# Local attention by token halves, two heads a step, with half of the output projection moved beside it

## The chip, the core and the metric

The kernel runs on one core of one Trainium2 chip. The time is the device time of one launch in microseconds, and the number compared is the median over several runs. The engines are called by the names of the profile: PE (TensorE, with PEld for its weight loads), DVE (VectorE), ACT (ScalarE), POOL (GpSimd) and SP (SyncE, which here only starts transfers).

## What is computed

One decoder layer over 512 tokens of width 1024, in float32. The part that matters here is the end of the attention block and the start of the feed-forward block:

```python
mix = concatenate([moba, nsa, diff, swa], axis=-1)   # 4 groups of 4 heads of 64
x = x + rms_norm(mix @ w_out, attn_post_norm)
h = rms_norm(x, ffn_pre_norm)
x = x + rms_norm(conv_ffn(h, w_gate, w_up, ...), ffn_post_norm)
```

`swa` is attention over a band: a query sees itself and the 127 tokens before it, there are two key/value heads for four query heads, and a learned "sink" joins the maximum and the sum of each softmax row. With query tiles of 128 tokens, tile i needs the key tiles i-1 and i; tile 0 needs only key tile 0.

## The kernel before

Every float32 operand of a matmul is split into a high and a low part, and a product is three matmuls (`mm3`, lines 405 to 407: high by high, high by low, low by high). The split costs an ACT copy and a DVE or POOL subtraction for each block; for weights these are `Weights.operand` (lines 191 and 194, tiles `wu`, and `wa` for the first two operands of the feed-forward block) and `Weights.plain` (152, 157). Line 177 is a sum or difference of weight blocks on POOL, made for a seven-product (Strassen) form of the gate and up projections, and it overwrites blocks that the splits of `wa` read.

Attention is written as a list of tasks, one for each head (swa, moba), head and branch (nsa) or head pair (diff). A task has steps: scores of a query tile with the softmax exponent (line 948 on DVE, 949 on ACT), `end` (row sums, reciprocal, normalisation on POOL, line 941), `transposes` (PE 973, ACT 976, DVE 977), and `pv` (values; for swa line 1139). After `pv`, `fold` adds two partial results (ACT 994, DVE 995) and, after every second head, `mix_pair` splits the mixed output into `mixT` (ACT 999, POOL 1000). The steps are sorted by a hand-written due time. Between them a generator, `everything()`, supplies projection work in pieces of three matmuls (`fill`, `advance`): first the input projections, last `fill_out`, the half of the output projection whose inputs are the moba and nsa heads (k = 0 to 3), kept in eight tiles `part[t][n]` (four token tiles t, two column halves n).

After the last swa task the second half of the output projection follows: `out_rest(t, n)` (12 matmuls in a PSUM bank, tags `mm` and `sc`, then a DVE addition into `part`, line 1217), for t = 0, 1, then `second_norm(0)` and `second_norm(1)`, then t = 2, 3 and their norms. `second_norm` is: two squares with row sums on ACT (1225), a scalar on DVE (1228), a power on POOL (1231), a product with the gain (1241, POOL except for t = 0), the residual addition into `x1` (1244, DVE), again square, scalar (1230) and power, and the second gain (1247, DVE). `right_operand` transposes the result (PE 1257) and splits it (ACT 1259, DVE 1260). Two operands of the first token half ("11", "21") feed the four products of `first_products` (lines 1312 to 1314, 24 matmuls each); all others need both halves and come from differences (1284).

A scheduler of the framework orders the instructions of each engine by a simulated time with the program order as priority; a `high_priority` block raises the priority. Tiles of one tag are handed out in the order in which the program asks for them. The tag "H" has 16 tiles: the normalised input, later `mixT` 4 to 7 and `wa`. The pool `fp`, which holds `x1`, uses the memory of the attention pools and so can be written only after the last swa task has read its probabilities.

## Time and profile before

| | us |
|---|---|
| median of 3 runs | 822.89 |
| lowest, highest run | 821.38, 822.95 |
| the profiled execution, its own time | 821.32 |
| its span (first to last instruction) | 819.5 |

The profile shows one execution. Busy time of an engine is the sum of its instructions; a bracket with an arrow in a timeline is idle time of the engine before the instruction, and what ended it. The mean granted TensorE clock over the span was 0.984 of full speed.

### The profile page before, as it was taken

The page shows a single profiled execution, that of the slowest core. Times are in us where ns is not written, and L with a number is a line of the kernel's source. Part 1 is how long each engine was busy: PE and PEld are TensorE (multiplying, and loading weights), DVE is VectorE, ACT ScalarE, POOL GpSimd, SP SyncE. Part 2 cuts the span into 40 slices and gives each one's busy share as a digit, 9 for nine tenths or more (in the row PEclk, how much of TensorE's full clock was granted, in tenths as well). Part 3 has the DMA queues.
Part 4 walks back from the last instruction along what each step waited for, and adds up shares of the span by engine and source line. Part 5 has one row for each costly group of instructions (what it writes and reads, how often), then busy time and mean ns, then how long its engine had stood idle before and what let it go on. Part 6 is the DMA issues. An engine that isn't in the chain of part 4 may idle for free.

```text
span 819.5 us, 13505 instructions
## 1 busy us (share of the span) xinstructions
PE 781.0 (95%) x5087; PEld 712.1 (87%) x5087; DVE 665.6 (81%) x1131; ACT 446.9 (55%) x931; POOL 338.5 (41%) x309
## 2 busy tenths in 40 slices
PE   8999998999989769999999999999999999999995
PEld 8998986997868658988998998998998998998984
DVE  5657768877586999896797797897897987989857
ACT  6657666777676545645554453454454454445532
POOL 5245333336244757343343441461561561563103
PEclk9999999999989979999999999999999999999998
DMA  7455201416211403412114305216116026033212
GB/s 213 121 149 138 64 22 46 129 52 216 80 52 52 154 7 109 145 61 94 52 50 157 103 10 197 67 38 206 43 61 206 18 86 205 1 104 104 69 60 102
DMA packets 72920, 78.76 MB, mean 96 GB/s; under 512 B 7782, under 2 KB 58136, under 8 KB 72856
## 3 DMA queue, kind: packets, MB, share of 16 engines
q1 hardware_dynamic: 71032, 73.71, 29.3%
q10 hardware_dynamic: 1824, 4.20, 1.5%
q8 instruction: 40, 0.66, 0.3%
q14 instruction: 24, 0.20, 0.1%
HBM read 73.71 MB, written 2.10 MB: 93 GB/s over the span
## 4 chain that ended last, share of the span: by engine, by line
PE 57%; DVE 33%; issue 3%; DMA 3%; ACT 2%; POOL 1%; ACTq 0%; DVEq 0%; POOLq 0%
DVE wu L194 13%; PE mm L405 5%; PE mm L406 5%; PE mm L407 4%; DVE y L1362 3%; PE mm L1312 3%; PE mm L1314 3%; PE mm L1313 3%; PE tr L406 3%; PE tr L407 2%; PE sc L1314 2%; PE sc L1313 2%; PE sc L1312 2%; PE tr L405 2%; PE tr L973 2%
## 5 line engine op out<-in xcount | busy, mean ns | idle before, releaser
L194 DVE TENSOR_TENSOR wu<-pair,wu 128x512 fp32r<-128x512 f32 x188 | 174.6, 964 | 15.8 <-ACT wu L191 15.6
L191 ACT ACTIVATE wu<-pair 128x512 fp32r<-128x512 f32 x188 | 108.6, 622 | 76.3 <-PE sc L1314 19.8
L1314 PE MATMUL mm<-fT,wu 128*128 128x256 f32 x488 | 138.3, 283 | 0.7 <-DVE wu L194 0.7
L1312 PE MATMUL mm<-fT,wu 128*128 128x256 f32 x488 | 138.2, 283 | 0.7 <-ACT mo L1343 0.7
L1313 PE MATMUL mm<-fT,wu 128*128 128x256 f32 x488 | 138.2, 283 | 0.0
L1314 PE MATMUL sc<-fT,wu 128*128 128x256 f32 x392 | 111.3, 284 | 0.0
L1313 PE MATMUL sc<-fT,wu 128*128 128x256 f32 x392 | 111.1, 284 | 0.0
L1312 PE MATMUL sc<-fT,wu 128*128 128x256 f32 x392 | 111.0, 284 | 0.0
L152 ACT ACTIVATE wu<-raw 128x512 fp32r<-128x512 f32 (+2 forms) x126 | 71.3, 609 | 67.9 <-DMA raw<-in_ffn_w_down_dram 43.8
L177 POOL TENSOR_TENSOR sum<-pair 128x512 f32<-128x512 f32 x32 | 48.7, 1526 | 141.2 <-DMA pair<-in_ffn_w_up_dram 71.4
L177 POOL TENSOR_TENSOR pair<-sum,pair 128x512 f32<-128x512 f32 x32 | 56.2, 1771 | 116.6 <-DVE wu L194 114.7
L177 POOL TENSOR_TENSOR pair<-pair 128x512 f32<-128x512 f32 x64 | 103.4, 1628 | 2.0
L157 DVE TENSOR_TENSOR wu<-raw,wu 128x512 fp32r<-128x512 f32 (+2 forms) x96 | 73.5, 783 | 35.3 <-ACT wu L152 34.8
L1312 PEld LDWEIGHTS mm<-fT,wu 128*128 128x128 f32 x488 | 93.6, 192 | 1.2 <-ACT mo L1343 0.9
L1314 PEld LDWEIGHTS mm<-fT,wu 128*128 128x128 f32 x488 | 93.6, 192 | 0.9 <-DVE wu L194 0.9
L1313 PEld LDWEIGHTS mm<-fT,wu 128*128 128x128 f32 x488 | 93.6, 192 | 0.3
L941 POOL TENSOR_SCALAR P<-P,rc 128x128 f32<-128x128 f32 (+2 forms) x80 | 42.3, 547 | 84.3 <-DVE rc L1039 39.6
L1313 PEld LDWEIGHTS sc<-fT,wu 128*128 128x128 f32 x392 | 75.2, 192 | 0.3
L1312 PEld LDWEIGHTS sc<-fT,wu 128*128 128x128 f32 x392 | 75.2, 192 | 0.3
L1314 PEld LDWEIGHTS sc<-fT,wu 128*128 128x128 f32 x392 | 75.3, 192 | 0.0
L949 ACT ACTIVATE P<-P,mn 128x128 f32<-128x128 f32 (+2 forms) x96 | 52.1, 543 | 33.2 <-DVE mn L948 32.8
L157 POOL TENSOR_TENSOR wu<-raw,wu 128x512 fp32r<-128x512 f32 (+2 forms) x30 | 40.6, 1356 | 48.4 <-ACT wu L152 44.7
(318 smaller groups left out, 1955.8 us busy)
## 6 DMA issues: line engine op xcount, KB each, us to landing
pair<-in_ffn_w_gate_dram SPq DMA_DIRECT2D x16, 1024.0 KB, 7.7
pair<-in_ffn_w_up_dram SPq DMA_DIRECT2D x16, 1024.0 KB, 5.4
raw<-in_ffn_w_down_dram SPq DMA_DIRECT2D x32, 512.0 KB, 4.1
raw<-in_w_in_dram SPq DMA_DIRECT2D x14, 512.0 KB, 3.9
raw<-in_w_out_dram SPq DMA_DIRECT2D x8, 512.0 KB, 5.4
raw<-in_w_in_dram SPq DMA_DIRECT2D x10, 256.0 KB, 3.2
x<-in_x_dram SPq DMA_DIRECT2D x4, 512.0 KB, 4.6
x<-in_x_dram ACTq DMA_DIRECT2D x4, 512.0 KB
```

The costliest lines, as they stand in the source:

```text
L152: keep(self.nc.scalar.activation(box["h"][:, sl], box["r"][:, sl], AF.Copy))
L157: keep(eng.tensor_tensor(box["l"][:, sl], box["r"][:, sl], f32(box["h"][:, sl]), op=ALU.subtract))
L177: self.nc.gpsimd.tensor_tensor(block(g, out), block(g, a), block(g, b), op=op)
L191: self.nc.scalar.activation(box["h"][g], block(g, src), AF.Copy)
L194: self.nc.vector.tensor_sub(box["l"][g], block(g, src), f32(box["h"][g]))
L405: pe.matmul(o, lh, rh, start=first, stop=False)
L406: pe.matmul(o, lh, rl, start=False, stop=False)
L407: pe.matmul(o, ll, rh, start=False, stop=last)
L949: act.activation(pi, pi, AF.Exp, bias=mn[:, i:i + 1], scale=-1.0, accum_out=sm[:, i:i + 1])
L1312: pe.matmul(o, wh, rh, start=first, stop=False, skip_group_check=True)
L1313: pe.matmul(o, wh, rl, start=False, stop=False, skip_group_check=True)
L1314: pe.matmul(o, wl, rh, start=False, stop=last, skip_group_check=True)
```

## The change

The four swa tasks are now pairs (token half, pair of heads) in the order (0,0), (0,1), (1,0), (1,1): each does two query tiles of two heads. Scores, exponents and normalisation keep their shapes; `end` uses two small activations for the sinks; the transposes are 3 + 3 tiles for the first token half and 4 + 4 for the second; `pv` puts both heads into one PSUM bank; the folds are 64 rows by 256 columns, and the mixed output is split by halves of 256 tokens, the last one on DVE. After the pair (0,1) the filler goes on with `fill_rest`: it loads the residual input of token tiles 0 and 1 through SP into four "H" tiles, takes the four weight units of `out_rest`, and yields the pieces of `out_rest` for t = 0, 1, with their additions put into the queue of side work. `x1` is loaded from memory only for t = 2, 3, and `second_norm(0)` and `(1)` read the early copy. `out_rest` uses the `mm` banks alone. For t = 2, 3 it runs after the attention, as before.

```diff
--- before.py
+++ after.py
@@ -885,18 +885,45 @@
                 mm_done()
         yield "out"
 
+    def out_rest(t, n):
+        ps = mm_bank()
+        sl = slice(128 * t, 128 * t + 128)
+        for k in range(4):
+            w = late["wo"][2 * n + k // 2]
+            mm3(ps, mixT[0][4 + k][:, sl], mixT[1][4 + k][:, sl], w[0][:, k % 2, :], w[1][:, k % 2, :], k == 0, k == 3)
+            yield 1
+        later(lambda: vec.tensor_add(part[t][n], part[t][n], ps))
+        mm_done()
+
+    def fill_rest():
+
+        late["x"] = [[f32(tt("xm", "H")) for _ in range(2)] for _ in range(2)]
+        for t in range(2):
+            for n in range(2):
+                sp.dma_start(late["x"][t][n], x[0, 128 * t:128 * t + 128, 512 * n:512 * n + 512])
+        late["wo"] = [W.take() for _ in range(4)]
+        for n in range(2):
+            for t in range(2):
+                yield from out_rest(t, n)
+        yield "rest"
+
     def everything():
         yield from fill_moba()
         yield from fill_nsa()
         yield from fill_diff()
         yield from fill_swa()
         yield from fill_out()
+        while not late.get("half"):
+            yield "wait"
+        yield from fill_rest()
 
     filler = everything()
     seen = set()
 
     def advance():
         y = next(filler, None)
+        if y == "wait":
+            return None
         if isinstance(y, str):
             later(lambda: seen.add(y))
         elif y is not None and side:
@@ -1106,42 +1133,63 @@
         t.pv = pv
         return t
 
-    def swa_task(h):
+    def swa_task(half, p):
+
         t = Task()
-        p, a = h // 2, h % 2
         box = []
-        score = stacked_score(sq_[h], sk[p], late["skl"][p])
-
-        def one(i):
-            if i == 0:
-                box.append(new_probs())
-            P, mn, sm = box[0]
-            probs(score, slope(3, h), i, P, mn, sm, SOFF, SN, sbias[:, 256 - SN[i]:256], 128 * max(i - 1, 0),
-                  nsink[:, h:h + 1])
-        t.first = [lambda i=i: one(i) for i in range(4)]
+        ns = ((128, 256), (256, 256))[half]
+        w = ns[0] + ns[1]
+        at = [w * (j // 2) + ns[0] * (j % 2) for j in range(4)]
+
+        def one(j):
+            if j == 0:
+                box.extend(new_probs())
+            P, mn, sm = box
+            a, i, n = j // 2, 2 * half + j % 2, ns[j % 2]
+            ps = bank("sc")
+            stacked_score(sq_[2 * p + a], sk[p], late["skl"][p])(ps, i, 128 * max(i - 1, 0), n)
+            pi = P[:, at[j]:at[j] + n]
+            vec.tensor_tensor_reduce(pi, ps[:, 0:n], sbias[:, 256 - n:256], slope(3, 2 * p + a),
+                                     nsink[:, 2 * p + a:2 * p + a + 1], ALU.add, ALU.min, mn[:, j:j + 1])
+            act.activation(pi, pi, AF.Exp, bias=mn[:, j:j + 1], scale=-1.0, accum_out=sm[:, j:j + 1])
+        t.first = [lambda j=j: one(j) for j in range(4)]
 
         def end():
-            t.P, mn, sm = box[0]
+            t.P, mn, sm = box
             es = st1.tile([128, 4], F32, tag="es", name=nm("es"))
-            act.activation(es, mn, AF.Exp, bias=sink[:, h:h + 1])
+            for a in range(2):
+                h = 2 * p + a
+                act.activation(es[:, 2 * a:2 * a + 2], mn[:, 2 * a:2 * a + 2], AF.Exp, bias=sink[:, h:h + 1])
             vec.tensor_add(sm, sm, es)
-            normalise(t.P, recip(sm), SOFF, SN)
+            normalise(t.P, recip(sm), at, ns + ns)
         t.end = end
-        t.srcs = SWA
+        t.srcs = [[w * a + 128 * n for n in range(w // 128)] for a in range(2)]
 
         def pv():
             o = bank("pv")
             v = vcs["s"]
-            for j, c, n, first in ((0, 0, 256, True), (1, 0, 128, False), (2, 0, 256, True), (1, 128, 128, False),
-                                   (3, 0, 128, False)):
-                for b in range(2):
-                    oc = 128 * j + c
-                    pe.matmul(o[:, oc:oc + n], v[:, j, p, 64 * a:64 * a + 128],
-                              t.pt[b][:, 256 * j + c:256 * j + c + n], start=first and b == 0,
-                              stop=not first and b == 1, skip_group_check=True)
-            fold(o, h, 3)
-            if a:
-                mix_pair(mos[3], 6 + p)
+            mo = ta("mo", MO)
+            steps = (((0, 0, 256, 0), (1, 128, 128, 256)), ((2, 0, 256, 128), (1, 0, 128, 0), (3, 128, 128, 384)))[half]
+            for a in range(2):
+                for n, (j, c, m, pc) in enumerate(steps):
+                    for b in range(2):
+                        pe.matmul(o[:, 256 * a + c:256 * a + c + m], v[:, j, p, 64 * a:64 * a + 128],
+                                  t.pt[b][:, w * a + pc:w * a + pc + m], start=n == 0 and b == 0,
+                                  stop=n == len(steps) - 1 and b == 1, skip_group_check=True)
+            tmp = ta("tmp", TMP)
+            for a in range(2):
+                r, c = 64 * a, slice(256 * a, 256 * a + 256)
+                act.activation(tmp[r:r + 64, 0:256], o[64 - r:128 - r, c], AF.Copy)
+                vec.tensor_add(mo[r:r + 64, 0:256], o[r:r + 64, c], tmp[r:r + 64, 0:256])
+            if half == 0:
+                mixT[0][6 + p], mixT[1][6 + p] = tt("mixh", "H"), tt("mixl", "H")
+            c = slice(256 * half, 256 * half + 256)
+            act.activation(mixT[0][6 + p][:, c], mo[:, 0:256], AF.Copy)
+            (vec if half and p else pool).tensor_tensor(mixT[1][6 + p][:, c], mo[:, 0:256], f32(mixT[0][6 + p][:, c]),
+                                                        op=ALU.subtract)
+            if p and not half:
+                fill_to("out")
+                late["half"] = True
         t.pv = pv
         return t
 
@@ -1151,7 +1199,7 @@
             (None, moba_task, [(h,) for h in range(4)], RATES[0], "moba"),
             ("nsa", nsa_task, [(h, b) for h in range(4) for b in range(2)], RATES[1], None),
             ("diff", diff_task, [(h,) for h in range(4)], RATES[2], None),
-            ("swa", swa_task, [(h,) for h in range(4)], RATES[3], None)):
+            ("swa", swa_task, [(a, p) for a in range(2) for p in range(2)], RATES[3], None)):
         for n, ar in enumerate(args):
             box = {}
 
@@ -1193,28 +1241,18 @@
         cur = rate or cur
         with tc.high_priority(HP):
             f()
-    fill_to("out")
+    fill_to("rest")
     ph_cm.__exit__(None, None, None)
     first_half.close()
 
 
     fp = ctx.enter_context(tc.tile_pool(name="fp", bufs=1))
     x1 = [fp.tile([128, D], F32, name=f"x1_{t}") for t in range(4)]
-    for t in range(4):
+    for t in (2, 3):
         act.dma_start(x1[t], x[0, 128 * t:128 * t + 128, :])
     t2pool = ctx.enter_context(tc.tile_pool(name="t2", bufs=XB))
     gpost, gpre = gains[0][:, 0, :], gains[0][:, 1, :]
-
     flush()
-    ws = [W.take() for _ in range(4)]
-
-    def out_rest(t, n):
-        ps = bank(("mm", "sc")[n])
-        sl = slice(128 * t, 128 * t + 128)
-        for k in range(4):
-            w = ws[2 * n + k // 2]
-            mm3(ps, mixT[0][4 + k][:, sl], mixT[1][4 + k][:, sl], w[0][:, k % 2, :], w[1][:, k % 2, :], k == 0, k == 3)
-        vec.tensor_add(part[t][n], part[t][n], ps)
 
     def rstd2(*src):
 
@@ -1241,7 +1279,7 @@
             eng.tensor_tensor(part[t][n], part[t][n], half_of(gpost, n), op=ALU.mult)
         for n in range(2):
             xh = half_of(x1[t], n)
-            vec.scalar_tensor_tensor(xh, part[t][n], r, xh, ALU.mult, ALU.add)
+            vec.scalar_tensor_tensor(xh, part[t][n], r, late["x"][t][n] if t < 2 else xh, ALU.mult, ALU.add)
         r = rstd2(x1[t])
         for n in range(2):
             vec.scalar_tensor_tensor(part[t][n], half_of(x1[t], n), r, half_of(gpre, n), ALU.mult, ALU.mult)
@@ -1265,11 +1303,12 @@
 
     R = {}
     for half in range(2):
-        for n in range(2):
-            for t in (2 * half, 2 * half + 1):
-                out_rest(t, n)
-            if half:
+        if half:
+            for n in range(2):
+                for t in (2, 3):
+                    run(out_rest(t, n))
                 W.free(2)
+            flush()
         for t in (2 * half, 2 * half + 1):
             with tc.high_priority(HN):
                 second_norm(t)
```

## Rows read from the trace of the kernel before

**Rows 1.** The profile's first part: the span, and the busiest two engines with busy time, share of the span and instructions.

```profile
span 819.5 us, 13505 instructions
PE 781.0 (95%) x5087; PEld 712.1 (87%) x5087; DVE 665.6 (81%) x1131; ACT 446.9 (55%) x931; POOL 338.5 (41%) x309
```

**Rows 2.** Busy time by stretch of the span. Columns: the stretch, its length, then busy us (and instructions) of PE, PEld, DVE, ACT and POOL, the granted TensorE clock, the share of the DMA engines, GB/s.

```profile
234.00:250.00 16.00, 14.17 (x68) 10.89 (x69) 13.93 (x56) 11.96 (x39) 6.18 (x12) 0.79 0.18 54
250.00:263.00 13.00, 11.42 (x82) 9.98 (x81) 8.90 (x23) 7.87 (x23) 7.09 (x12) 1.00 0.25 78
263.00:268.60 5.60, 5.60 (x32) 4.79 (x31) 1.38 (x3) 3.07 (x6) 2.30 (x2) 1.00 0.27 78
268.60:282.60 14.00, 13.60 (x59) 10.61 (x57) 13.97 (x18) 9.54 (x21) 11.89 (x10) 1.00 0.51 194
282.60:298.00 15.40, 4.33 (x18) 3.10 (x17) 15.40 (x23) 6.08 (x14) 8.40 (x8) 0.67 0.01 1
298.00:307.50 9.50, 8.47 (x67) 8.06 (x67) 9.50 (x15) 3.01 (x6) 4.71 (x4) 1.00 0.08 15
307.50:326.00 18.50, 17.09 (x141) 16.51 (x141) 18.50 (x23) 11.05 (x21) 15.66 (x10) 1.00 0.27 84
...
340.00:819.50 479.50, 466.76 (x3175) 432.15 (x3173) 406.46 (x530) 228.72 (x406) 183.42 (x120) 0.99 0.29 94
```

**Rows 3.** The longest wait between 235 and 315 us: who waited for whom, us in total, times, longest.

```profile
PEld tr L1257 <- DVE part L1247: 12.2, 3, 7.0
```

**Rows 4.** PE in order of time: the last matmul of `out_rest`, and the first transpose that needs both token halves. Columns: start, us, engine, line, output and inputs, shapes, count.

```profile
282.24 0.39 PE L407 MATMUL sc<-wu,mixl 128*128 128x512 f32 x1
...
307.56 0.30 PE L1257 MATMUL tr<-ident,part 128*128 128x128 f32 x1 [0.80 <-DVE part L1284]
```

**Rows 5.** DVE in order of time, around the end of the attention: instructions with idle time before them.

```profile
256.46 0.60 DVE L1100 COPY tmp<-dr 128x512 f32<-128x512 f32 x1 [1.42 <-POOL dr L1099]
...
261.04 1.16 DVE L977 TENSOR_TENSOR PT<-tr,PT 128x512 fp32r<-128x512 f32 x2 [1.37 <-ACT PT L976]
...
264.31 0.68 DVE L995 TENSOR_TENSOR mo<-vb,tmp 64x512 f32<-64x512 f32 x1 [1.39 <-ACT tmp L994]
266.15 0.69 DVE L995 TENSOR_TENSOR mo<-va,tmp 64x512 f32<-64x512 f32 x1 [1.16 <-ACT tmp L994]
268.59 2.05 DVE L194 TENSOR_TENSOR wa<-pair,wa 128x512 fp32r<-128x512 f32 x3 [1.75 <-ACT wa L191]
```

**Rows 6.** DVE in order of time, the norm of the first token half: the scalar and the residual additions of t = 0 and t = 1, and the last gain of t = 1 (counts of 2 are the two column halves).

```profile
274.27 1.25 DVE L1228 SCALAR_TENSOR_TENSOR r<-ss 128x1 f32<-128x1 f32 x1
...
276.65 3.40 DVE L1244 SCALAR_TENSOR_TENSOR x<-part,r,x 128x512 f32<-128x512 f32 x2
...
284.62 1.40 DVE L1244 SCALAR_TENSOR_TENSOR x<-part,r,x 128x512 f32<-128x512 f32 x2
...
294.22 1.41 DVE L1247 SCALAR_TENSOR_TENSOR part<-x,r,gains 128x512 f32<-128x512 f32 x2
```

**Rows 7.** POOL in order of time: the first and the last of the four weight differences that wait for the splits of `wa`.

```profile
270.72 1.28 POOL L177 TENSOR_TENSOR pair<-sum,pair 128x512 f32<-128x512 f32 x1 [1.83 <-DVE wa L194]
...
277.76 1.74 POOL L177 TENSOR_TENSOR pair<-pair 128x512 f32<-128x512 f32 x1
```

**Rows 8.** Groups of instructions between 268 and 310 us, shapes kept apart: line, engine, operation, names, shapes, count, busy us, mean ns, idle before.

```profile
L1247 DVE SCALAR_TENSOR_TENSOR part<-x,r,gains 128x512 f32<-128x512 f32 x8 | 8.6, 1129 | 0.0
L1244 DVE SCALAR_TENSOR_TENSOR x<-part,r,x 128x512 f32<-128x512 f32 x8 | 7.5, 989 | 0.0
...
L194 DVE TENSOR_TENSOR wu<-pair,wu 128x512 fp32r<-128x512 f32 x6 | 4.3, 757 | 0.0
...
L194 DVE TENSOR_TENSOR wa<-pair,wa 128x512 fp32r<-128x512 f32 x4 | 2.7, 721 | 1.7 <-ACT wa L191 1.7
...
L1217 DVE TENSOR_TENSOR part<-part,mm 128x512 f32<-128x512 f32 x4 | 2.6, 680 | 0.0
```

**Rows 9.** Groups of instructions between 230 and 268 us, in the same columns: the pieces of the swa tasks whose shape or number changes, and the score step in two widths.

```profile
L1000 POOL TENSOR_TENSOR mixl<-mo,mixh 128x512 fp32r<-128x512 f32 x4 | 5.1, 1284 | 6.7 <-ACT mixh L999 6.7
...
L948 DVE CUSTOM_DVE_ANT_0 P<-sc,sbias,nsink 128x256 f32<-128x256 f32 x12 | 5.7, 478 | 1.7 <-PE sc L1006 1.7
...
L995 DVE TENSOR_TENSOR mo<-va,tmp 64x512 f32<-64x512 f32 x3 | 2.1, 695 | 1.2 <-ACT tmp L994 1.2
...
L994 ACT ACTIVATE tmp<-va 64x512 f32<-64x512 f32 x3 | 1.8, 591 | 1.4 <-PE va L1139 1.3
...
L948 DVE CUSTOM_DVE_ANT_0 P<-sc,sbias,nsink 128x128 f32<-128x128 f32 x4 | 1.4, 345 | 0.3 <-PE tr L973 0.2
...
L1126 ACT ACTIVATE es<-mn,sink 128x4 f32<-128x4 f32 x4 | 1.1, 283 | 0.0
```

**Rows 10.** The end of the attention on ACT's queue, in order of time: the first two loads of the residual input, and the copies of `wa`.

```profile
265.59 0.96 ACTq L1204 DMA_DIRECT2D x<-in_x_dram  x2
...
267.93 2.20 ACT L191 ACTIVATE wa<-pair 128x512 fp32r<-128x512 f32 x4 [0.41 <-issue]
```

**Rows 11.** SP's queue in order of time: the weight load that waits for the last swa task.

```profile
265.52 0.37 SPq L104 DMA_DIRECT2D pair<-in_ffn_w_up_dram  x1
```

## The prediction

> **What bounds the kernel now.** I read the first part of the page first. PE is busy for 95% of the span and DVE for 81% [rows 1], so over the whole kernel PE looks like the bound. The change touches only the seam between attention and feed-forward, so the next view is busy time by stretch [rows 2]. The reader is to see a change of regime there. Up to 268.6 us and again after 340, PE is nearly full (466.76 of the last 479.5 us) and DVE has gaps. Between 268.6 and 326 it is the other way round: DVE is busy for 13.97 of 14.00, 15.40 of 15.40, 9.50 of 9.50 and 18.50 of 18.50 us, while PE is busy for only 4.33 of the 15.40 us from 282.6 to 298. PE's hole there is 11.1 us, with 1.0 more up to 307.5. The granted clock in the hole is 0.67, between the two levels (1.2 and 2.4 GHz); after it, it is full again.
>
> The waits say what PE wants in the hole: the transposes of line 1257 wait for line 1247, the last step of the norm [rows 3]. PE in order of time gives the two ends: `out_rest` ends at 282.6, and the first transpose that needs both token halves starts at 307.56 [rows 4]. So the seam costs what DVE's list costs. A microsecond is gained here only if DVE does something before 268.6 that it now does behind it, or does it faster. The room for that is on DVE itself: five gaps between 255 and 268.6, 1.42 + 1.37 + 1.39 + 1.16 + 1.75 = 7.1 us, of which the last three, 4.3 us, lie behind 263 [rows 5].
>
> **The change part by part.** *The swa tasks by halves.* Scores, exponents, transposed tiles (28) and value matmuls (40) keep their number and total width, so they cost nothing new. The folds go from 4 of 64x512 to 8 of 64x256 on both engines. The score step takes 345 ns for 128 columns and 478 for 256, 133 ns for 128 more [rows 9]; by this slope a DVE fold of 256 columns takes 695 - 266 = 0.43 us, and eight take 3.4 where four took 2.8: +0.65 us (bounds: nothing if it halves, +2.8 if it does not shrink). ACT pays about the same by its 591 ns, and 4 x 0.283 = 1.1 us more for the sink activations [rows 9]; ACT is busy for 7.87 of 13.00 and 3.07 of 5.60 us there [rows 2], so this stays hidden. Without that cover 1.8 us would be on the path. The last low part goes from POOL (1284 ns at full width) to DVE: the nearest DVE subtraction, `wa`, takes 721 ns at 512 columns [rows 8], by the same slope 0.45 (bounds 0.36 and 0.72). Together DVE gets +1.1 us (bounds 0.4 and 3.5).
>
> *`out_rest` of the first half as filler.* PE's matmuls are the same. PE is full from 263 to 268.6 and for 13.60 of the next 14.00 us [rows 2], and the first half's last input (the fold of pair (0,1)) comes only around 260, so I expect `out_rest` as a whole to end at 281 to 282.6, hardly earlier. What moves is DVE's additions: those of the first column half (two of 0.68 us, rows 8) get into the gaps: -1.4 us (bounds 0, and -2.7 for all four). Using two banks instead of four can hold PE for an addition of 0.68 us up to four times; PE's hole behind 282.6 covers it.
>
> *What the filler drags along.* While the pieces are emitted, the side queue is emptied too. In it stand the splits of `wa`. Now they start at 267.93, just behind the last head's split [rows 10], because their "H" tiles are asked for after all of `mixT`; in the new order the last `mixT` tiles are asked for at pair (0,1). Four DVE subtractions of `wa`, 2.7 us [rows 8], can so move ahead of 268.6 (bounds 0 and -2.7). With the two additions that makes 4.1 us, and the gaps behind 263 hold 4.3 [rows 5]: it just fits, so I take it whole.
>
> *POOL's differences.* Four instructions of line 177 wait for those splits, from 270.72 to about 279.5, 1.28 to 1.74 us each [rows 7]. In that time DVE needs 3.40 us for two residual additions that take 1.40 for two at 284.62, and 1.25 us for a scalar of one column [rows 6]. If the four go ahead with the splits, I expect DVE to win back one such collision in two: the 2.0 us of the two residual additions (bounds 0 and -4).
>
> The Trainium skill ("SBUF — State Buffer", section "SBUF: two separate sides") says why: VectorE and GpSimd share a port pair under an exclusive lock, and a VectorE instruction with two SBUF inputs waits for a whole GpSimd one. This speaks against the change as well: the subtractions of `wa` have two SBUF inputs too, so by that rule the collision moves along with them, the relief is nothing and the sum below would be 3.0 instead of 5.0.
>
> *The early residual input.* The loads of all four x tiles start at 265.59 on ACT's queue [rows 10]; two of them become four half loads on SP, which need free "H" tiles from about 262. SP also holds the weight load that waits for the last swa task and starts at 265.52 [rows 11]; if they end up behind it they start as late as now. Now the data is there at 276.65 at the latest, when line 1244 uses it [rows 6]; I expect 1244 for t = 0 at about 271, so the worst case costs some 5 us on that chain, of which DVE, with other work in its list, would lose 1 to 2. I take nothing. `x1` still cannot be written before the last swa task is through.
>
> **The sum.** DVE behind 263: -4.1 moved, +1.1 added, -2.0 relief = -5.0 us. The transpose at 307.56 [rows 4] should then start at about 302.5. The first half's norm is ready earlier by more than this (1244 at 271, not 276.65), so the first four products start at about 283 to 287, not 298. But they take PE only about 9 us, and the hole opens again in front of the operands of both halves: 282.6 to 302.5 is 19.9 us, with 4.33 + 8.47 = 12.8 us of PE work [rows 2], leaving 7 of the 12. Behind 326 nothing changes, and the 5 us are carried to the end. The profiled execution took 821.3 us and becomes 816.3; the median of the runs is 1.6 above it, so I predict 817.9.
>
> **The rivals.** *The hole closes further.* If POOL disturbs the norm much less, the excess over 0.70 us in lines 1247 and 1244, 8 x 0.43 + 8 x 0.29 = 5.7 us [rows 6, 8], goes instead of 2.0, and if the scheduler also lets the second half's norm pass some weight splits (six of `wu`, 4.3 us, in rows 8) the gain reaches 8.7 to 12; at 10 the time is 812.9. For it: PE has room for it, and the first half's norm gets free early. Against it: DVE's list is conserved, and POOL still has its own part of the norm.
>
> *Nothing moves.* If the tiles, or the raised priority of the swa steps, keep `wa` and the additions behind 268.6, only the order inside a full DVE list changes: 0 +- 1.6 us, 822.9. For it: the gaps are four of about 1.4 us, each behind a chain step. Against it: DVE takes its work in the scheduler's time order, and the gaps are twice as long as one instruction.
>
> *Slower: the moved work stands in front of the attention's last steps.* DVE and POOL run in order and do not interrupt. Between 255 and 268.6 the tail of the attention is a chain (scalar, transposed split, fold, low part). If each of the six moved DVE instructions holds a step of it for its 0.7 us, and two of POOL's differences of up to 1.74 us stand in front of a low part, the chain ends 7.6 us later, and the rest of the seam with it: +2.6 against the 5.0 gained, 825.5. It decides from 5 us of delay on. For it: PE is full behind 263, so late steps cost at once. Against it: only two or three steps are left by then.
>
> **How the numbers follow.** Forecast (gain of 2 to 8 us, own range 815 to 821): 0.57; hole closes further: 0.13; nothing moves: 0.14; slower: 0.16. About 0.2%, or 1.65 us, can be told from no change. Faster is 0.57 + 0.13 = 0.70, same 0.14, slower 0.16. The range 811.5 to 824.5 leaves out the far part of the closing hole (0.06) and the far part of the slower case (0.09).
>
> **What would show it.** Right: DVE in order of time has `wa` and at least two additions of `out_rest` before 268.6, and gaps there of under 3 us in all; the first products start at 283 to 287; PE has a hole of about 7 us right before the first transpose of both halves, at about 302; DVE is full up to some 321. Wrong: `wa` still behind 267 (nothing moves); the last value matmul of swa at 270 or later (slower); the residual addition of t = 0 waiting for a transfer; or PE with less than 3 us of hole between 270 and 320 (closes further). The forecast fails as a whole if DVE shows gaps behind 270, for then its list is not what sets the seam.

## The result: 832.5 us, 1.2% slower

The changed kernel takes 832.5 us (median of 4 runs, 830.68 to 833.11) against 822.85 for the kernel before on the same chip: ratio 1.0118, 95% interval 1.0098 to 1.0137. 817.9 was predicted, with 811.5 to 824.5 as range. The profiled execution took 830.68 us.

The page's first part, to set against [rows 1]: all engines are as busy as before to within 5 us, DVE and POOL less. What was added is idle time.

```profile
span 828.9 us, 13535 instructions
...
PE 783.0 (94%) x5087; PEld 715.1 (86%) x5087; DVE 662.9 (80%) x1136; ACT 448.5 (54%) x941; POOL 333.5 (40%) x310
```

Busy time of the changed kernel in the stretches of [rows 2], same columns:

```profile
250.00:263.00 13.00, 10.65 (x52) 9.88 (x53) 6.08 (x16) 5.94 (x17) 6.62 (x10) 0.61 0.16 55
263.00:268.60 5.60, 5.60 (x38) 5.03 (x38) 4.10 (x9) 4.45 (x11) 1.48 (x2) 1.00 0.00 0
268.60:282.60 14.00, 12.59 (x56) 10.10 (x55) 9.61 (x16) 7.15 (x19) 12.01 (x10) 1.00 0.43 150
282.60:298.00 15.40, 4.64 (x21) 3.52 (x19) 13.59 (x20) 6.86 (x16) 6.23 (x6) 0.80 0.22 69
298.00:307.50 9.50, 5.42 (x20) 3.93 (x20) 9.19 (x13) 4.49 (x8) 6.91 (x6) 0.60 0.01 2
307.50:326.00 18.50, 16.95 (x131) 16.95 (x132) 12.73 (x19) 6.39 (x12) 12.56 (x9) 0.91 0.18 58
```

DVE is the third busy time of a row. It was full from 268.6 to 326 in [rows 2]; now it works for 9.61 of 14.00 and 12.73 of 18.50 us. Work did move forward (4.10 us instead of 1.38 from 263 to 268.6), and what it left behind stands empty. PE's hole is longer and later; it shows in the waits from 235 to 325 us (who waits for whom, total, times, longest; the row of [rows 3] is the first):

```profile
PEld tr L1295 <- DVE part L1285: 14.1, 3, 12.8
PE tr L1295 <- DVE r L1268: 12.3, 1, 12.3
```

PE in order of time, as in [rows 4]: the end of `out_rest` (all eight groups, for both token halves), the first transpose behind it, and the first that needs both halves. The last has moved from 307.56 to 318.15, by 10.6 us; the span is 9.4 us longer, so the whole loss lies ahead of that point.

```profile
286.86 0.39 PE L407 MATMUL mm<-wu,mixl 128*128 128x512 f32 x1
...
299.59 0.48 PE L1295 MATMUL tr<-ident,part 128*128 128x128 f32 x1 [12.35 <-DVE r L1268]
...
318.15 0.27 PE L1295 MATMUL tr<-ident,part 128*128 128x128 f32 x1
```

Two things are late ahead of that hole. The first is the early residual input. SP's queue in order of time, and the wait of its load:

```profile
267.80 0.37 SPq L104 DMA_DIRECT2D pair<-in_ffn_w_up_dram  x1
285.06 1.77 SPq L903 DMA_DIRECT2D xm<-in_x_dram  x4
```

```profile
SPq L903 <- PE mm L406: 17.1, 2, 16.8
```

The load waits 16.8 us for matmuls of `out_rest` (lines 405 to 407), that is, for `mixT` tiles to come free. The "H" tag has 16 tiles: `mixT` 4 to 7 take 8, and `wa` takes 8 (two units, high and low, two tiles each). Pair (0,1) first empties the side queue, `wa` asks for its 8, and `xm`, written ahead of the weights "early", finds none. The `mixT` tiles that it then waits for hold both token halves. So the load for the first half waits until `out_rest` of the second half has read them as well; it starts behind a matmul of the last of the eight groups:

```profile
284.59 0.39 PE L406 MATMUL mm<-wu,mixh 128*128 128x512 f32 x1
```

DVE in order of time shows the subtractions of `wa` and the second thing that is late, the end of the attention:

```profile
266.33 0.42 DVE L1183 TENSOR_TENSOR mo<-vb,tmp 64x256 f32<-64x256 f32 x1 [0.96 <-ACT tmp L1182]
266.78 1.29 DVE L194 TENSOR_TENSOR wa<-pair,wa 128x512 fp32r<-128x512 f32 x2
268.10 0.43 DVE L1183 TENSOR_TENSOR mo<-vb,tmp 64x256 f32<-64x256 f32 x1
268.56 1.30 DVE L194 TENSOR_TENSOR wa<-pair,wa 128x512 fp32r<-128x512 f32 x2
269.89 1.29 DVE L895 TENSOR_TENSOR part<-part,mm 128x512 f32<-128x512 f32 x2
271.09 0.41 DVE L1183 TENSOR_TENSOR mo<-va,tmp 64x256 f32<-64x256 f32 x1
271.95 0.43 DVE L1183 TENSOR_TENSOR mo<-va,tmp 64x256 f32<-64x256 f32 x1 [0.45 <-ACT tmp L1182]
272.86 0.42 DVE L1188 TENSOR_TENSOR mixl<-mo,mixh 128x256 fp32r<-128x256 f32 x1 [0.48 <-ACT mixh L1187]
...
276.55 0.16 DVE L1266 SCALAR_TENSOR_TENSOR r<-ss 128x1 f32<-128x1 f32 x1 [0.85 <-ACT junk L1263]
...
288.20 0.74 DVE L1282 SCALAR_TENSOR_TENSOR x<-part,r,xm 128x512 f32<-128x512 f32 x1
```

The scalar of t = 0 starts at 276.55, only 2.3 us behind [rows 6]; its residual addition (1282) runs at 288.20, behind the load. And the last low part of `mixT` ends at 273.28. In the kernel before it ended at 268.89, on POOL:

```profile
267.59 1.30 POOL L1000 TENSOR_TENSOR mixl<-mo,mixh 128x512 fp32r<-128x512 f32 x1 [2.64 <-ACT mixh L999]
```

Four subtractions of `wa` and two additions of `out_rest` stand between the last folds.

### The profile page after: what moved, and what is told of

Its sections match the earlier page's. It is cut to its first block, busy times and chain, and to the rows that moved or that the text cites. A ratio compares the mean times of both kernels' runs of the same rounds, so it can differ in the third digit from the quotient of the medians.

```text
span 828.9 us, 13535 instructions
## 1 busy us (share of the span) xinstructions
PE 783.0 (94%) x5087; PEld 715.1 (86%) x5087; DVE 662.9 (80%) x1136; ACT 448.5 (54%) x941; POOL 333.5 (40%) x310
## 4 chain that ended last, share of the span: by engine, by line
PE 66%; DVE 24%; issue 3%; ACT 3%; DMA 2%; POOL 1%; DVEq 0%; POOLq 0%; SPq 0%; ACTq 0%
DVE wu L194 9%; PE mm L405 5%; PE mm L406 4%; PE mm L407 4%; PE mm L1352 4%; PE mm L1353 4%; PE mm L1351 4%; PE tr L406 4%; PE tr L407 3%; PE sc L1353 3%; PE sc L1352 3%; PE sc L1351 3%; PE tr L405 3%; DVE y L1401 3%; PE tr L1000 2%
## 5 line engine op out<-in xcount | busy, mean ns | idle before, releaser
L157 DVE TENSOR_TENSOR wu<-raw,wu 128x512 fp32r<-128x512 f32 (+2 forms) x96 | 75.3, 802 | 35.7 <-ACT wu L152 35.1
L976 ACT ACTIVATE P<-P,mn 128x384 f32<-128x384 f32 (+2 forms) x80 | 44.5, 557 | 31.7 <-DVE mn L975 31.2
```

The source lines that it names most:

```text
L157: keep(eng.tensor_tensor(box["l"][:, sl], box["r"][:, sl], f32(box["h"][:, sl]), op=ALU.subtract))
L976: act.activation(pi, pi, AF.Exp, bias=mn[:, i:i + 1], scale=-1.0, accum_out=sm[:, i:i + 1])
```

## Experiments: which of the two costs what

Losses below are the ratio to the kernel before, less one, times 822 us. Times within a kernel are those of its one profiled execution.

**x from free tiles.** The whole change, with x in a tag that has room:

```
-        late["x"] = [[f32(tt("xm", "H")) for _ in range(2)] for _ in range(2)]
+        late["x"] = [[f32(tt("xm")) for _ in range(2)] for _ in range(2)]
```

> The changed kernel, with the four early half tiles of x taken from the tag F (18 tiles, whose attention operands are released during the swa tasks) instead of H. Theory A (the early x is late, because its H tiles come free only when out_rest has used mixT): the loads start before 268 us instead of 285, the residual addition of t = 0 goes from 288.2 to about 278 us, right behind its scalar, PE's hole behind out_rest (287 to 304) shrinks to under 5 us, and the time is 820 to 824 us. Theory B (the regrouped attention and the reordered out_rest, which ends at 287 instead of 282.6 us, are themselves the loss): less than half of the 9.6 us comes back, the time stays above 828 us.

825.68 us, ratio 1.0050 (1.0034 to 1.0067): the loss falls from 9.7 to 4.1 us. This lies between the two expectations. The last two of the four loads now start 39 us earlier (SP's queue):

```profile
245.80 1.78 SPq L903 DMA_DIRECT2D xm<-in_x_dram  x2
```

**No early x.** The whole change, but x of all four token tiles loaded into `x1` on ACT's queue as before (`for t in range(4)`).

> The changed kernel without the early load: x1 is loaded for all four token tiles on ACT's queue as before, at about 268 us. Theory A: four loads land by about 277 us, the scalar of t = 0 is there at 277.7, so the time is within 2 us of the run with the tag F, 820 to 825 us. If the early load itself is worth something, this run is slower than that one by the wait for the loads, 1 to 3 us. Theory B: above 828 us.

826.38 us, 1.0053 (1.0033 to 1.0072), which cannot be told from the experiment above. A timely early load is worth nothing that shows here; a late one costs.

**The late x alone.** The kernel before, x of t = 0, 1 on SP into "H" tiles asked for behind `wa`:

```
-    for t in range(4):
+    for t in (2, 3):
         act.dma_start(x1[t], x[0, 128 * t:128 * t + 128, :])
...
+    late["x"] = [[f32(tt("xm", "H")) for _ in range(2)] for _ in range(2)]
+    for t in range(2):
+        for n in range(2):
+            sp.dma_start(late["x"][t][n], x[0, 128 * t:128 * t + 128, 512 * n:512 * n + 512])
...
-            vec.scalar_tensor_tensor(xh, part[t][n], r, xh, ALU.mult, ALU.add)
+            vec.scalar_tensor_tensor(xh, part[t][n], r, late["x"][t][n] if t < 2 else xh, ALU.mult, ALU.add)
```

> The kernel before, with only the load of x for t = 0, 1 replaced: four H tiles asked for behind those of mixT and wa, on SP. Theory A: the loads start only when the last bank of out_rest has read mixT 4, at about 281 us, the residual addition of t = 0 goes from 276.65 to about 284 us, and the time rises by 4 to 9 us, to 827 to 832. Theory B: DVE has other work in that time (its list was full), within 2 us of 822.9.

829.95 us, 1.0102 (1.0087 to 1.0117): +8.4 us with nothing else changed. SP's load, and on DVE the addition that needs it:

```profile
281.14 1.76 SPq L1212 DMA_DIRECT2D xm<-in_x_dram  x4
```

```profile
287.43 0.74 DVE L1248 SCALAR_TENSOR_TENSOR x<-part,r,xm 128x512 f32<-128x512 f32 x1
```

So the first cause is shown, and it would make 8.4 of the 9.7 us alone. The 4.1 us that the whole change still loses with x in time are not its remainder, since they stay when it is gone.

**The regrouped attention alone.** The kernel before with the new `swa_task` and its task list, and neither `fill_rest` nor the early x.

> The kernel before with the regrouped swa tasks alone (pairs of token half and head pair); the output projection, the loads of x and the norms as before. Theory A: the regrouping costs 0 to 3 us (the last value matmul of swa was at 267.8 instead of 265.5 us in the changed kernel), 822 to 826 us. Theory B: most of the 9.6 us is here, above 828 us.

832.25 us, 1.0132 (1.0117 to 1.0147): +10.9 us, more than the whole change with timely x. The last low part ends at 277.34, and behind the seam a second hole opens. PE and DVE in order of time:

```profile
323.25 1.11 PE L1275 MATMUL tr<-ident,t 128*128 128x128 f32 x4 [6.38 <-DVE fT L1278]
```

```profile
315.83 3.42 DVE L194 TENSOR_TENSOR wu<-pair,wu 128x512 fp32r<-128x512 f32 x2
319.17 0.67 DVE L1351 TENSOR_TENSOR c<-tmp,sc 128x512 f32<-128x512 f32 x1
319.77 2.82 DVE L194 TENSOR_TENSOR wu<-pair,wu 128x512 fp32r<-128x512 f32 x2
322.51 0.68 DVE L1278 TENSOR_TENSOR fT<-tr,fT 128x512 fp32r<-128x512 f32 x1
```

PE has transposed and waits 6.38 us, because the split of its result (1278) stands in DVE's queue behind four weight splits, which take 3.42 and 2.82 us for two.

Set beside each other, the runs give a sum. The regrouped attention alone loses 10.9 us, with the moved projection beside it (no early x) 4.4, and with the late x on top 9.7. So the moved projection gave back some 6.5 us, and the late x took some 5.3 of them away again; the intervals leave each of these differences uncertain by about 2 us.

**Heads in another order.** The kernel before with swa heads 2, 3, 0, 1, a control for "any reordering of attention upsets the schedule".

> The kernel before with its four swa tasks, one for each head, in the order 2, 3, 0, 1. The work, the shapes and the due times are the same; only which head pair comes first changes. If the cost of the regrouping lies in its shapes and numbers (theories C and D), this run is within 2 us of the kernel before, 820 to 823.5. Theory E (the scheduled order at this seam is fragile, any change of it costs several us): more than 3 us away from 821.4.

821.52 us, 0.9989 (0.9975 to 1.0004): no change. The schedule stands this reordering.

**Four banks** for `out_rest` (on the first experiment), `mm` and `sc` as before the change.

> The run with x in the tag F, with out_rest on the mm banks for the first column half and on the sc banks for the second, as in the kernel before. If the two banks cost what PE waits for the additions (one gap of 1.42 us before 272.82), the time falls by 0 to 1.5 us, 824 to 826; if PE was waiting for other things there anyway, no change within 1 us.

831.03 us, 1.0113 (1.0096 to 1.0129): 5 us worse than the first experiment, with the second hole (6.4 us). Going back to four banks is no gain, so the two banks are not what the change loses by.

## Experiments: why the attention ends late

In the first experiment the last score starts when it did before (250.16 against 250.26), but the power of the differential heads' norm starts at 257.18 (before 254.77), the last value matmul of swa at 268.48 (264.24), and the last low part ends at 275.46 (268.89). Each experiment takes one suspect.

**POOL's normalisation in front of the power.** First experiment, with the second half's normalisation on DVE:

```
-    def normalise(p, r, offs, ns):
+    def normalise(p, r, offs, ns, eng=pool):
...
-            pool.tensor_scalar(pi, pi, r[:, i:i + 1], 0.0, ALU.mult, ALU.add)
+            eng.tensor_scalar(pi, pi, r[:, i:i + 1], 0.0, ALU.mult, ALU.add)
...
-            normalise(t.P, recip(sm), at, ns + ns)
+            normalise(t.P, recip(sm), at, ns + ns, vec if half else pool)
```

> The run with x in the tag F, with the normalisation of the two second-half swa tasks (8 instructions of 128x256) on DVE instead of POOL. Theory C (what is left of the loss is a later end of the attention, and it begins on POOL: both second-half normalisations, 3.67 us, stand in front of the power of the last diff pair, which starts at 257.2 instead of 254.8 us): the power starts by 255.7, the last part of mixT is ready by 273 instead of 275.5, and the time falls from 825.7 to 822 to 824. Theory D (the folds in single file through one buffer are the delay): the power may be earlier, the last part of mixT moves by less than 1 us, the time stays within 1 us of 825.7.

828.39 us, 1.0087 (1.0065 to 1.0108). POOL is free, and the power still starts only at 256.90, behind the scalar that it needs (line 1125, 256.66). The product that this scalar reads (line 1123, on PE) ends at 256.55: PE's queue holds it behind transposes that wait 1.94 us for the normalisation, now on DVE, and it takes 1.71 us at a granted clock of 0.50, where it took 0.95 in the kernel before at 1.00. The first experiment has the same order on PE, with the scalar waiting 2.04 us for line 1123, so POOL's queue was not what held the power:

```profile
253.79 1.60 PE L1000 MATMUL tr<-ident,P 128*128 128x128 f32 x6 [2.14 <-POOL P L968]
255.19 1.70 PE L1123 MATMUL vb<-pair,tmp 128*128 128x2 f32 x8
```

**The sink exponentials.** The kernel before with each of them in two (128x2), and the first experiment with one per step (DVE adds a broadcast tile of sinks, ACT does one exponential):

> The kernel before, with one thing changed: each sink exponential of local attention is two activations of 128x2 instead of one of 128x4. ScalarE gets four instructions of about 0.28 us more, 1.1 us, two of them in the stretch 246 to 255 where it has no gap in the kernel with the change. Theory S (ScalarE's extra instructions push the differential heads' tail back): the POOL power of that tail goes from 254.8 to 255.3 to 256, and the time up by 0.5 to 1.1 us. Theory F (the half folds in single file at the end) and theory R (regrouping itself: a step is complete only with both of its heads, and the last one holds 1024 columns): no change, within 0.4 us.

> The whole change with x in free F tiles (the first experiment), and one sink exponential per step: VectorE adds a broadcast 128x4 tile of sinks to the minima (about 0.1 us), ScalarE does one activation instead of two. Theory S: the power comes back from 257.2 to about 256 and the time falls 0.5 to 1.2 us below that experiment's 825.7. Theories F and R: within 0.5 us of 825.7.

821.98 us, 1.0007 (0.9995 to 1.0019), and 827.5, 1.0071 (1.0049 to 1.0093). The second brings the power back to 255.41, but the last low part stays at 275.37: the power's result now waits behind two transposed splits on DVE. ACT's extra work was hidden, as predicted.

**The folds in halves.** The kernel before, each fold as two of 64x256:

> The kernel before, with one thing changed: each fold of local attention (ScalarE copy, VectorE addition, 64x512) is done as two halves of 64x256, four folds becoming eight. Theory F: each head's fold becomes a chain of four instructions of about 0.43 to 0.48 us instead of two of about 0.7, with a hand-over between each, so the last low part moves from 268.9 to about 269.5 to 271 and the time up by 0.6 to 2 us. Theories S and R: within 0.4 us of the kernel before.

824.12 us, 1.0027 (1.0013 to 1.0041). The last low part ends 1.1 us later, counted from the last score, and the loss is 2.2 (1.1 to 3.4). This part of the regrouping has a price by itself.

**Tiles for the folds' copies.** A step's two half folds share one tile, and ACT's second copy waits for DVE's first addition (0.44 to 0.55 us). Four kernels on the first experiment or on the regrouped attention alone: two tiles (`TMP = 2`); two tiles and one for each half fold (`tmp = ta("tmp", TMP)` inside the loop); the same with one sink exponential; and the regrouped attention alone with them.

> The whole change with x in free F tiles (the first experiment), and two tiles for the copies of the folds instead of one. That tile also holds the squares of the differential heads' norm, so in the first experiment the first folds of local attention wait until that norm is through, and the second pair's folds wait for the first's. Theory F: last local attention product from 268.5 to 265 or 266, last low part from 275.5 to 272 or 273, time 2 to 3 us below 825.7. Theories S and R: the same within 0.5 us, since what is late is released by the softmax before it.

> The whole change with x in free F tiles (the first experiment), the copies' tiles doubled as in the previous one, and each half fold with a tile of its own. Until now the two half folds of a step shared one tile, and ScalarE's second copy waited for VectorE's first addition (0.44 to 0.55 us each), so that doubling the tiles between steps could not unlock a step. Theory F in this narrower form: the four instructions of a step overlap, 0.9 us less for each step, last local attention product at 266 to 267 instead of 268.5, last low part at about 272.5 to 274 instead of 275.5, time 1 to 2.5 us below 825.7. Theory R (the step is late for what stands before its folds, and what follows sets the time): last low part moves less than 1 us, time 825 to 831, like the two-tile kernel.

> The kernel of the line before with one sink exponential per step. If ScalarE's extra instructions and the single file together make the tail late, this is the earliest of the regrouped kernels: power at about 255.4, last low part at 271 to 273, time 822 to 824. If neither matters, it is 825 to 831.

> The regrouped local attention alone (the fourth experiment, 832.3), with a copy tile for each half fold. Theory F: last low part from 277.3 to 274 or 275, and if the second hole of TensorE (6.4 us in 310 to 330) follows from the late end, it shrinks too: 826 to 829. If the hole is set by the order in which VectorE's list was written and not by the time at which attention ends, it stays and the time is 830 to 832.

831.18 (1.0122), 830.45 (1.0102), 831.68 (1.0112) and 831.06 (1.0104). The first three lose 8 to 10 us where the first experiment loses 4.1; the fourth loses 8.6 against 10.9 without the tiles, with intervals that overlap. So none is better by a margin that can be told. The third is the clearest. Its last value matmul starts at 266.69, early among these kernels (2.4 us later than before, counted from the last score), and its last low part ends at 275.04 all the same. DVE there, in order of time:

```profile
268.87 0.42 DVE L1183 TENSOR_TENSOR mo<-va,tmp 64x256 f32<-64x256 f32 x1
269.30 0.69 DVE L194 TENSOR_TENSOR wa<-pair,wa 128x512 fp32r<-128x512 f32 x1
269.92 1.27 DVE L895 TENSOR_TENSOR part<-part,mm 128x512 f32<-128x512 f32 x2
271.11 0.79 DVE L194 TENSOR_TENSOR wa<-pair,wa 128x512 fp32r<-128x512 f32 x1
271.93 0.43 DVE L1183 TENSOR_TENSOR mo<-va,tmp 64x256 f32<-64x256 f32 x1
272.40 1.21 DVE L1279 TENSOR_TENSOR part<-part,gains 128x512 f32<-128x512 f32 x1
273.53 1.51 DVE L1188 TENSOR_TENSOR mixl<-mo,mixh 128x256 fp32r<-128x256 f32 x1
```

Two folds and a low part, 2.4 us of work (the low part takes 1.51 beside a weight difference on POOL), are spread over 6.2 us. Two subtractions of `wa`, two additions of `out_rest` and a product of the norm stand between them; the second fold's copy is there at 270.19, and the fold runs at 271.93. Another kernel, on the first experiment, takes the tile of each half fold from the "F" tag (`tmp = tf("tmp")` in the loop):

> The run with x in the tag F, with a buffer of its own (from the tag F) for each of the eight half folds, so that no fold waits for the square of the last diff pair or for the fold before it. Theory D: the first fold starts by 259 instead of 261.5 us, the last part of mixT is ready 2 to 3 us earlier, time 822 to 824. Theory C: the second value matmuls still wait for a PSUM bank that the diff pair holds, less than 1 us changes, 825 to 826.

828.32 us, 1.0092 (1.0055 to 1.0130). Its seven runs scatter from 825.83 to 834.79 us, and the trace is that of a run of 833.82. The last value matmul starts at 260.25, the last low part still ends at 275.34: ACT copies for the last four half folds only from 270.54 on, behind copies in its queue that wait for the projection on PE. With the order shifted so far, nothing follows from it for the tiles.

**A late end alone.** The kernel before with copies to and fro in front of the last mix, five times or twice. Five of them also keep DVE busy for 2.1 us and ACT for 3.1:

```
+            if a and p:
+                for _ in range(5):
+                    tmp = ta("tmp", TMP)
+                    act.activation(tmp, mos[3], AF.Copy)
+                    vec.tensor_copy(mos[3], tmp)
```

> The kernel before, with attention's end made late and nothing else: ahead of the last mix, its 128x512 tile is copied five times by ScalarE and back by VectorE in a chain (about 5 x 1.3 us; the values stay). The last low part moves from 268.9 to about 275.5, which is where the regrouped kernels have it. If a late end of attention is what costs the 4.3 us of the first experiment, this kernel loses 3.5 to 6.5 us (825 to 828). If the seam absorbs it and the regrouped kernels lose their time in the order of what stands behind, it loses under 1.5 us.

> The late-end kernel with two copies there and back instead of five, 2.25 us instead of 5.6. If a late end costs one for one, this one loses 2 to 3 us (823.5 to 825.5). If most of the loss of the five-copy kernel is a jump of the order behind (VectorE's list written in another order once the end is late enough), it loses either under 1 us or most of the 8.

831.69 us, 1.0097 (1.0067 to 1.0126), and 825.47, 1.0046 (1.0024 to 1.0068): 5.6 us of lateness cost 8.0 (3.5 to 6.5 were expected), and 2.2 us cost 3.8. POOL's last low part in the five-copy kernel, and what PE then waits for from 270 to 310:

```profile
275.42 1.28 POOL L1000 TENSOR_TENSOR mixl<-mo,mixh 128x512 fp32r<-128x512 f32 x1 [8.24 <-ACT mixh L999]
```

```profile
PE tr L1262 <- DVE part L1252: 12.3, 3, 8.7
PE mm L405 <- ACT mixh L999: 4.9, 1, 4.9
```

**An earlier end.** The kernel before with `TMP = 2`, so that the first folds need not wait for the differential norm.

> The kernel before with two tiles for the folds' copies instead of one, and nothing else. If the end of attention sets the time one for one in both directions, unlocking the first folds from the differential norm (they start at 258.4 because its tile is read until 258.3) brings the last low part from 268.9 to about 267.5 to 268.5 and the time down by 0.4 to 1.4 us, which would beat both kernels. If TensorE's order (twelve output products ahead of the last local attention product at 264.2) already hides it, no change, within 0.4 us.

822.84 us, 1.0010 (0.9996 to 1.0023). Counted from the last score the end did not move (18.77 us; before 18.63), so this tells nothing of an earlier end, and no kernel of the study is faster than the one before by more than its interval.

All of it in one table. Lateness is the end of the last low part counted from the start of the last score matmul, less the 18.63 us of the kernel before; PE is its busy time from 310 to 330 us, where the regrouped kernels have their second hole. The last two kernels show no hole there because theirs lies ahead of 310 (12.35 and 15.49 us, then 3.46 in each), and their first products fall into the window.

| kernel | end late by, us | PE of 20 us | loss, us |
|---|---|---|---|
| before | 0 | 19.14 | 0 |
| heads 2, 3, 0, 1 | 0.0 | 19.09 | -0.9 |
| sinks in two | -0.3 | 19.00 | 0.6 |
| before, two tiles | 0.1 | 19.06 | 0.8 |
| folds in halves | 1.1 | 18.57 | 2.2 |
| late end, two copies | 2.2 | 19.31 | 3.8 |
| late end, five copies | 5.6 | 17.21 | 8.0 |
| x in free tiles | 6.7 | 15.88 | 4.1 |
| no early x | 6.6 | 16.55 | 4.4 |
| one sink exponential | 6.0 | 15.94 | 5.8 |
| norm on DVE | 6.1 | 16.35 | 7.2 |
| tiles and one sink | 6.1 | 13.56 | 9.2 |
| tiles from "F" | 13.6 | 13.16 | 7.6 |
| two tiles | 7.3 | 13.19 | 10.0 |
| own tiles | 7.9 | 12.00 | 8.4 |
| regrouped alone, own tiles | 8.1 | 12.34 | 8.6 |
| regrouped alone | 8.0 | 12.20 | 10.9 |
| four banks | 8.4 | 12.19 | 9.3 |
| late x alone | 0.0 | 20.00 | 8.4 |
| the change | 6.2 | 20.00 | 9.7 |

Every kernel that ends the attention in time is level, except the one with the late x; every regrouped one ends it 6 to 8 us late and loses (13.6 with the tiles from "F", whose last score matmul starts at 243.08, 5 us ahead of all others). The loss is no simple multiple of the lateness: of the kernels with x in time that are 6 to 8 us late, those with a small second hole (PE busy for about 16 of the 20 us) lose 4 to 7 us and those with a large one (12 to 14) 8 to 11, and two that differ only in the tiles lie 6 us apart.

What stays open is why the regrouped attention ends late. Sinks and tiles are excluded as single causes, moving the normalisation left PE waiting for it as before, and the halved folds explain 1.1 us of 6 to 8. For the rest there is only what the traces show, an engine's queue with other work in front of the next step: `wa` and additions on DVE with the moved projection; in the regrouped attention alone PE's queue, where the last value matmul (270.89) stands behind 16 matmuls of the projection (12 in the kernel before). None of this was tested by itself, and the moved work can't be the whole cause: the regrouped attention alone moves none of it and ends 8.0 us late, later than with it (6.6). Nor was it tried whether the last step's 1024 columns, against 896 for a head before, matter.

## Why the prediction was wrong

*"I take nothing" for the early x: failed.* I costed the worst case at "some 5 us on that chain", of which DVE would lose 1 to 2, by assuming that the load would at worst queue behind SP's weight load at 265.52 [rows 11]. I did not count the tiles. The filler that I expected to pull `wa` forward is the one that takes x's tiles, and I had said that it empties the side queue. The load waited 16.8 us for tiles. A load made late in this way costs 8.4 us in the kernel before, and some 5.3 in the changed one. My sign for it came out, too: the residual addition of t = 0 runs 11.7 us behind its scalar, after a load that starts at 285.06.

*"DVE's list is conserved, and sets the seam": failed.* The sum turned 5.0 us of moved DVE work into 5.0 us of time. That holds only if DVE never waits. The list was full before because its inputs happened to be ready; with the attention's end and x late, DVE stood still for 4.4 of 14.00 and 5.8 of 18.50 us. My own sign for this, gaps behind 270, came out, and the first products, forecast for 283 to 287, start at 304.37.

*"wa" and two additions before 268.6: half right.* Two of four subtractions of `wa` start at 266.78, the others at 268.56, the additions at 269.89. They did not fall into gaps, they stood between the last folds.

*The slower rival saw the late end, with the wrong price and a cause that is not shown.* It set the delay against a gain of 5.0 us, one for one, and wanted 7.6 us of it for 825.5. The two late-end kernels show 1.4 to 1.7 us lost for each us, so that from 3 to 3.5 us on the gain would have been gone; the attention ended 6.2 us late. It blamed the moved work, and the regrouped attention ends late without that work too. Its sign, the last value matmul at 270 or later, did not come out (266.30). Counted from the last score (248.47; 250.26 before), that matmul is 3.9 us later than before and the last low part 6.2, so 2.3 us of the delay arise in the folds behind it.

*Regrouping: +1.1 us. The term that was furthest off.* Alone it costs 10.9. The sizes were right, a fold of 256 columns takes 0.43 us and the low part 0.42. The mistake was to count them as work to be added to a list, when they are links of a chain whose end everything behind waits for. The halved folds are 2.2 of the 10.9; what makes up the rest stays open.

*POOL's differences: -2.0 us, failed.* In the changed kernel the residual additions of t = 0 take 0.74 us each (3.40 for two in [rows 6]), but they run 11.6 us later than before, and two `wu` splits at 281.18 take 1.97 us beside line 1279 on POOL. With x in time (the first experiment) they take 3.40 again:

```profile
280.01 3.40 DVE L1282 SCALAR_TENSOR_TENSOR x<-part,r,xm 128x512 f32<-128x512 f32 x2
```

There the differences have ended by 278.32, and line 1279 on POOL, from 279.87 on, stands in their place. The relief was nothing, as the prediction said the rule would have it. That rule is the one from the Trainium skill ("SBUF — State Buffer", section "SBUF: two separate sides"), by which VectorE with two SBUF inputs waits for a whole GpSimd instruction that has begun before it; the trace agrees, with 3.42 us for two splits beside line 177 in the regrouped attention alone, where two take 1.28 us by themselves.

*Hidden, as predicted:* the sink exponentials (a difference of 0.6 us that can't be told from none) and the two banks (four are no faster).

## What to carry to other kernels

An early load is early only if its tile is free early: list who takes tiles of the tag ahead of it, in program order, before its cost is put at nothing. A stretch in which an engine is 100% busy shows that its inputs arrive in time, not that shortening its list shortens the stretch; ask what is late next if the producer slips by 2 us. Work moved into the gaps of a dependent chain can land between its links, as four subtractions and two additions did here, and a regrouped chain can end later with the same work; so price the chain's end and not the sum of work.

## What the hardware showed

I had not expected the clock to fall in the tail of the attention. In the changed kernel PE is busy for 1.88 of 4.00 us from 250 to 254, where before it had the first products of `out_rest` for the `sc` banks as filler (3.37). The granted clock goes to 0.50, the lower of its two levels, and stays there from 251 to 261. Two windows of the kernel before:

```profile
250.00:254.00 4.00, 3.37 (x23) 2.76 (x22) 3.26 (x11) 4.00 (x15) 1.50 (x5) 1.00 0.78 246
254.00:258.00 4.00, 3.13 (x26) 2.78 (x26) 2.32 (x7) 1.02 (x3) 4.00 (x7) 1.00 0.00 0
```

Windows of the changed kernel, columns as in [rows 2], and, in a fence of their own, two groups of eight value matmuls of the same shapes, the first in that stretch and the second behind it:

```profile
250.00:254.00 4.00, 1.88 (x9) 1.55 (x10) 2.50 (x8) 2.65 (x10) 2.42 (x6) 0.62 0.50 174
254.00:258.00 4.00, 3.77 (x17) 3.45 (x18) 0.69 (x3) 0.73 (x2) 2.92 (x4) 0.50 0.00 0
258.00:262.00 4.00, 4.00 (x24) 4.00 (x23) 2.63 (x5) 1.74 (x4) 0.72 (x1) 0.60 0.02 6
```

```profile
255.47 1.97 PE L1176 MATMUL vb<-PT,vs 128*128 128x256 f32 x8
...
261.10 1.15 PE L1176 MATMUL va<-PT,vs 128*128 128x256 f32 x8
```

The eight take 1.97 us at the lower level and 1.15 behind it. So a thinned-out PE makes the steps behind it longer as well as later. All regrouped kernels have such a stretch between the last score and the last value matmul, 3.4 to 10.2 us long in windows of 1 us; those by heads have none there. Yet the lateness does not follow its length: the regrouped attention alone ends 8.0 us late with 3.4 us of it, the change 6.2 us late with 10.2. How much of the 6 to 8 us is due to the clock, no run here isolates.
